# Reciprocals of softmax sums: through DRAM as rows, or spread and transposed

## The chip, the cores and the metric

The kernel runs on one core of a Trainium2 chip. The core has a matrix engine (PE, with its weight loads shown as PEld), a vector engine (DVE), a scalar engine (ACT), a general engine (POOL), and a queue that issues transfers (SP). They run side by side and wait for each other through semaphores. The metric is the device time of one execution in microseconds (us), the median over the runs; lower is better.

## The reference, cut to what matters

The program is one inference step of a two-layer encoder over 2048 prompt tokens and 64 sample tokens, with a model width of 1024. Layer 0 has two groups of heads side by side: A (eight heads, each query sees its own chunk of 64 tokens and all earlier ones) and B (eight heads, own chunk and the previous eight, with a learned bias by distance). Layer 1 has attention C (16 heads that share two key/value heads, own chunk and the previous two, with a learned sink per head). For all three:

```
p      = softmax(q k^T * scale + mask or bias)      # over the keys
o      = p v
mixed  = o * silu(gate)
h      = h + rmsnorm(mixed @ w_out) * g_post
```

The softmax is computed without its division: P = exp(s - max), and the sums of P over the keys are kept, one number per query and head. The division is made on o, at the end. This document is about how the reciprocals of these sums reach the shape in which o can be multiplied by them.

## The kernel before, in words

All work is float32. Products of high precision are built from a rounded part and a remainder, so most matmuls come in threes or pairs. The program runs five phases one after the other, with some overlap at the borders: phase 1 projects the input, phase 2 is attention A, phase 3 is attention B together with the output projection of layer 0, phase 4 projects the input of layer 1, phase 5 is attention C with the second output projection.

The scores of 128 queries lie with the queries on the 128 partitions. `exp` (L701, L1185, L1697) writes P and, as a side result, the sum of each row: one number per partition. P is then transposed block by block (L725, L1202, L1706), so that P V comes out with 64 head dimensions on partitions and queries along the free axis: `OT` holds two heads (2 x 64 partitions) by up to 512 queries. The sums therefore have their queries on partitions, while `OT` has them along the free axis.

Before, the turn is made like this. A reciprocal `ri` is taken of the sums of a group (four blocks of 128 queries, two heads, in A and B; one block of 128 queries, 16 heads, in C). A copy spreads each reciprocal 64 times along the free axis (`rb`: POOL L805 in A, ACT in B, ACT in C, POOL L1726 for the sample tokens in C). PE transposes `rb` in blocks of 128x128 (L810, L1245, L1735) into PSUM, where each of the two halves of 64 partitions now holds 64 equal rows: one head's reciprocals along the queries. DVE multiplies `OT` by that (L812, L1246, L1737). POOL multiplies by the gate `G` (L813, L1247, L1743). In A and B the result goes to DRAM (`sM`, `sMB`) for the output projection; in C it stays on chip and is split in a rounded part (`MM`, ACT) and a remainder (POOL L1750) for the projection (L963).

What sets the order of the work around it:

- In A (`finish` from L796) each group is a list of closures on the list `extra`. One entry is taken at the end of each step; a step is one block of queries of one head, or several short ones. Before, a group has two entries, `finish` and `rest`. For PE, DVE, ACT and POOL the order of the steps is written out by hand; SP's order is chosen by a planner that simulates the program. `rb` has one buffer. What is left on the lists after the last step is placed by the planner on all engines.
- In B (`finish` from L1230) each group is a generator in `J.side`. `J.rest()` resumes it once per unit (one block, one head), and once more when two or more wait. The loop `for _ in range(YR3 ...)` puts two or three turns between the spread copy and the transposes. PE, DVE, ACT and SP follow the written order; POOL is planned. The groups are `GROUPS = [(4, 4), (8, 4), (12, 4), (2, 2), (0, 2)]`, first block and count; the last two are short.
- In C (`gate` from L1715) each block of 128 queries is a generator in `J.side` too, with the same turns; the first eight steps are planned, and from then on PE, DVE, ACT and SP follow the written order, while POOL is planned. At most two blocks are open at a time (`J.open`).

The output projection's tail (L984 to L1005) runs between: DVE scales a row tile `z` by its norm and `g_post` (L994, two halves), POOL adds the residual (L1002), and SP stores it.

## Time and profile before

| | us |
|---|---|
| runs: median of 3 (lowest, highest) | 2731.71 (2725.06, 2732.81) |
| the profiled execution, its own time | 2735.98 |
| its span in the profile | 2733.9 |
| PE busy in the span | 2579.7 (94%) |
| DVE busy | 1473.2 (54%) |
| ACT busy | 1390.9 (51%) |
| POOL busy | 769.1 (28%) |

The profile shows one execution. Its span runs from the first to the last instruction and is 2.1 us shorter than the execution's own time. A group in it is a line of the code with an engine, an operation and the tiles it writes and reads (out<-in), the count after an x, the busy time, the mean duration in ns, and then the idle time of the engine just before, with what ended it. Rows with a time in front are single instructions or merged runs of them: start, length, engine, line. The chain of waits is followed back from the last instruction, at each step to what released it. "issue" in it is time in which the engine waited for nothing that the profile shows. Helper functions give their own line to all that they issue: L211 is every ACT copy, L214 every DVE remainder.

### The profile page before, as it was taken

To read this page: it belongs to the slowest core of one execution; us is meant where nothing else is said; L and a number is where in the kernel's file an instruction comes from. 1 tells how busy PE (TensorE), PEld (TensorE's weight loads), DVE (VectorE), ACT (ScalarE), POOL (GpSimd) and SP (SyncE) were. 2 spreads that over 40 slices of the span, in tenths; PEclk is the share of its full clock that TensorE was granted. 3 is DMA by queue.
4 is the path that set the end of the run, shared out by engine and by line. 5 is a ranking of instruction groups with operands and counts; after the bars stand their busy time and mean duration, and the time that the engine had idled before them with its cause. 6 is when DMAs were issued, how large, how long until landed. Compare 5 with 4: busy or idle time off the path is not lost.

```text
span 2733.9 us, 46704 instructions
## 1 busy us (share of the span) xinstructions
PE 2579.7 (94%) x16296; PEld 2355.2 (86%) x16296; DVE 1473.2 (54%) x4048; ACT 1390.9 (51%) x3547; POOL 769.1 (28%) x1311
## 2 busy tenths in 40 slices
PE   6999999999999999999988999899999999999997
PEld 6999999899998888888777888679999998787886
DVE  5542245352117878787666777545213204787884
ACT  4332242332237777777556666542233224777783
POOL 2123122113112323321200333374212220344444
PEclk9999999999999999999899999999999999999999
DMA  6456443737537666661476777666535429454552
GB/s 235 153 154 215 127 152 94 248 112 225 165 94 204 183 183 190 169 168 47 166 194 152 192 200 192 184 202 217 159 98 168 125 69 254 108 139 130 139 132 70
DMA packets 382283, 437.92 MB, mean 160 GB/s; under 512 B 49937, under 2 KB 308889, under 8 KB 378817
## 3 DMA queue, kind: packets, MB, share of 16 engines
q1 hardware_dynamic: 382048, 434.95, 54.7%
q8 instruction: 129, 2.11, 0.3%
q14 instruction: 106, 0.86, 0.1%
HBM read 282.80 MB, written 157.09 MB: 161 GB/s over the span
## 4 chain that ended last, share of the span: by engine, by line
PE 74%; DVE 11%; DMA 5%; ACT 5%; issue 3%; POOL 2%; SPq 1%; ACTq 0%; DVEq 0%; POOLq 0%
PE pm L237 36%; PE proj L963 9%; PE s L682 6%; PE acc L753 4%; PE t L725 3%; PE acc L1215 2%; DVE PT L214 2%; PE s L1175 2%; PE t L1202 2%; PE acc L1713 2%; PE t L1706 2%; PE s L1685 1%; ACT P L701 1%; DVE m L688 1%; DVE s L1688 1%
## 5 line engine op out<-in xcount | busy, mean ns | idle before, releaser
L237 PE MATMUL pm<-X,W 128*128 128x384 f32 (+2 forms) x4536 | 755.5, 325 | 1.4 <-DVE ev L214 1.0
L237 PEld LDWEIGHTS pm<-X,W 128*128 128x128 f32 x4536 | 734.9, 190 | 3.9 <-DVE ev L214 1.2
L211 ACT ACTIVATE PT<-t 128x512 fp32r<-128x512 f32 (+3 forms) x704 | 343.5, 504 | 265.5 <-PE t L1202 108.4
L214 DVE SCALAR_TENSOR_TENSOR PT<-t,PT 128x512 fp32r<-128x512 f32 (+3 forms) x688 | 375.5, 569 | 93.4 <-ACT PT L211 90.6
L963 PE MATMUL proj<-Wo,MM 128*128 128x512 f32 (+1 forms) x1368 | 379.5, 407 | 10.9 <-ACT z L211 8.8
L228 POOL TENSOR_TENSOR W<-R,W 128x768 fp32r<-128x768 f32 (+3 forms) x114 | 228.7, 2030 | 536.4 <-ACT W L227 536.1
L214 DVE SCALAR_TENSOR_TENSOR ev<-pm,ev 128x256 fp32r<-128x256 f32 (+3 forms) x197 | 98.7, 503 | 468.8 <-ACT ev L1553 169.3
L963 PEld LDWEIGHTS proj<-Wo,MM 128*128 128x128 f32 (+1 forms) x1368 | 237.1, 186 | 55.8 <-ACT z L211 12.4
L237 PE MATMUL pm<-W,X 128*128 128x256 f32 (+5 forms) x2040 | 281.1, 297 | 0.0
L237 PEld LDWEIGHTS pm<-W,X 128*128 128x128 f32 (+1 forms) x2040 | 271.7, 187 | 1.3 <-POOL W L228 0.3
L701 ACT ACTIVATE P<-s,m 128x512 f32<-128x512 f32 (+9 forms) x344 | 209.2, 616 | 32.8 <-DVE m L690 30.4
L682 PE MATMUL s<-KA,Q 128*128 128x512 f32 (+7 forms) x640 | 202.1, 398 | 9.7 <-ACT P L701 8.8
L725 PE MATMUL t<-ident,P 128*128 128x128 f32 x1088 | 177.0, 277 | 3.3 <-ACT P L701 0.8
L688 DVE TENSOR_REDUCE m<-s 128x1 f32<-128x480 f32 (+7 forms) x216 | 132.4, 613 | 82.3 <-PE s L682 81.9
L725 PEld LDWEIGHTS t<-ident,P 128*128 128x128 f32 x1088 | 135.4, 141 | 41.4 <-ACT P L701 15.0
L753 PE MATMUL acc<-PT,V 128*128 128x256 f32 x1152 | 156.0, 285 | 6.4 <-DVE OT L762 6.4
L753 PEld LDWEIGHTS acc<-PT,V 128*128 128x128 f32 x1152 | 140.4, 188 | 11.5 <-PE t L725 6.0
L1697 ACT ACTIVATE P<-s,m 128x256 f32<-128x256 f32 (+2 forms) x264 | 119.5, 465 | 10.6 <-DVE m L1689 9.3
L1688 DVE CUSTOM_DVE_ANT_0 s<-s,mask 128x256 f32<-128x256 f32 (+1 forms) x256 | 107.6, 422 | 20.2 <-PE t L1706 7.9
L1179 DVE CUSTOM_DVE_ANT_0 s<-s,bias 128x640 f32<-128x640 f32 (+4 forms) x128 | 95.1, 743 | 43.1 <-PE s L1175 41.8
L682 PE MATMUL s<-KR,Q 128*128 128x384 f32 (+6 forms) x320 | 116.7, 365 | 1.6 <-DMA Q<-sQR 1.6
L227 ACT ACTIVATE W<-R 128x768 fp32r<-128x768 f32 (+3 forms) x114 | 98.2, 909 | 38.0 <-DMA R<-in_ab_w_in_dram 19.5
(249 smaller groups left out, 4019.9 us busy)
## 6 DMA issues: line engine op xcount, KB each, us to landing
Q<-sQA SPq DMA_DIRECT2D x128, 128.0 KB, 3.2
sWO<-W SPq DMA_DIRECT2D x32, 512.0 KB, 3.8
Q<-sQB SPq DMA_DIRECT2D x128, 128.0 KB, 3.0
Wo<-sWO SPq DMA_DIRECT2D x16, 1024.0 KB, 9.0
Q<-sQC SPq DMA_DIRECT2D x32, 512.0 KB, 7.6
R<-in_ab_w_in_dram SPq DMA_DIRECT2D x40, 384.0 KB, 3.7
K<-sKB SPq DMA_DIRECT2D x56, 256.0 KB, 5.2
V<-sVB SPq DMA_DIRECT2D x24, 512.0 KB, 6.4
```

Source lines behind the costliest of these rows:

```text
L211: nc.scalar.activation(out, in_, AF.Copy)
L214: nc.vector.scalar_tensor_tensor(out, x, scale, hi, op0=ALU.mult, op1=ALU.subtract)
L228: nc.gpsimd.tensor_tensor(Wv[:, 1, k0:k1], Rv, Wv[:, 0, k0:k1], op=ALU.subtract)
L237: nc.tensor.matmul(ps, lhs(x, k), rhs(y, k), start=(j == 0), stop=(j == n - 1))
L682: nc.tensor.matmul(s[:r, :n], self.Q[:, x, self.qo:self.qo + r], rhs, start=(x == 0), stop=(x == 2))
L688: nc.vector.tensor_reduce(m[:r, j:j + 1], s[:r, :n], axis=AX.X, op=ALU.max)
L701: nc.scalar.activation(self.P[:r, o0:o0 + n], self.s.pop(j)[:r, :n], AF.Exp, bias=self.m[:r, 6:7], accum_out=acc)
L725: nc.tensor.transpose(t[:, b], self.P[:, (b0 + b) * 128:(b0 + b + 1) * 128], ident)
L753: nc.tensor.matmul(acc[:, (i // 2) % 2], H.V[:, b0 + b], PT[:, x, b], start=(b0 + b == 0 and x == 0), stop=(b0 + b == i and x == 1))
L963: nc.tensor.matmul(p, M[:, x, k, :r], W[k][:, y, cs], start=(k == k0 and t == 0), stop=(k == k1 - 1 and t == 2))
L1688: nc.vector.tensor_tensor_reduce(s[:, c, :w], s[:, c, :w], mk, 1.0, -3e38, ALU.add, ALU.max, m[:, 0, c:c + 1])
L1697: nc.scalar.activation(self.P[:, c, :w], self.s[:, c, :w], AF.Exp, bias=m[:, 1, c:c + 1], accum_out=m[:, 0, c:c + 1])
```

## The change

The reciprocals are no longer spread before the transpose. Two helpers are new. `to_rows` transposes the small block of reciprocals of a group (128 queries by up to 16 columns) once, copies the rows (8 or 16 by 128) out of PSUM on ACT, and stores them to a new scratch tensor in DRAM. `rows_to_halves` loads them back twice, once for each half of 64 partitions, with a stride of zero over the partitions, so that all 64 read the same row. `rb` then holds what the transposes held in PSUM before, but in SBUF.

In A a group has four entries on the list in place of two: `finish`, `rows`, `back`, `scale`. The last group (head pair 3, blocks 12 to 15) keeps the old form. In B the spread copy and the transposes go, and the turns are one, one and two. In C the reciprocals are taken one step earlier, in a new method `sums`, and a second list `J.recips` carries the row store and, one step later, the loads of `rb` and of `G`; `gate` then lets POOL multiply G by rb, and DVE multiply OT by that in one instruction of 128x1024, in place of two on DVE and then one on POOL. The sample tokens of C go the same way.

```
+    sRA = scratch("sRA", [4, 5, 8, 128])
+    sRB = scratch("sRB", [4, 6, 8, 128])
+    sRC = scratch("sRC", [17, 16, 128])
...
+    def to_rows(pool, pt, ri, n, dst):
+
+        p = pt.tile([128, 512], F32, name="t")
+        nc.tensor.transpose(p[:n, :128], ri, ident)
+        e = pool.tile([16, 128], F32, name="rT", bufs=1)
+        nc.scalar.activation(e[:n], p[:n, :128], AF.Copy)
+        dma(dst, e[:n])
+
+    def rows_to_halves(out, src, half, ap):
+
+        for e in range(2):
+            dma(out[e * 64:e * 64 + 64], bass.AP(tensor=src.tensor, offset=src.offset + e * half, ap=[[0, 64]] + ap))
...
-                rb = sc.tile([128, 4, 2, 64], F32, name="rb", bufs=1)
-                nc.gpsimd.tensor_copy(rb[:, :nb], ri[:, :nb, :, None].to_broadcast([128, nb, 2, 64]))
+                rb = sc.tile([128, 4, 128], F32, name="rb", bufs=1)
+                if (hp, b0) != (3, 12):
+                    sr = sRA[hp, b0 // 4, 0:2 * nb]
+
+                    def rows():
+                        to_rows(sc, ps_t, ri[:, :, :nb].rearrange("p e b -> p (e b)") if nb == 4 else ri[:, :, 0], 2 * nb, sr)
+
+                    def back():
+                        rows_to_halves(rb[:, :nb].rearrange("p b q -> p (b q)"), sr, nb * 128, [[1, nb * 128]])
+
+                    def scale():
+                        nc.vector.tensor_mul(OT[:, c0:c1], OT[:, c0:c1], rb.rearrange("p b q -> p (b q)")[:, :c1 - c0])
+                        nc.gpsimd.tensor_tensor(OT[:, c0:c1], OT[:, c0:c1], G[:, :c1 - c0], op=ALU.mult)
+                        dma(sM[hp * 128:hp * 128 + 128, c0:c1], OT[:, c0:c1])
+                    extra.extend([rows, back, scale])
+                    return
...
-                rb = sc.tile([128, 4, 2, 64], F32, name="rb", bufs=1)
-                copy(rb[:, :nb], ri[:, :nb, :, None].to_broadcast([128, nb, 2, 64]))
-                for _ in range(YR3 if t0 < 512 or t0 == SEQ else 2):
-                    yield
-                p = ps_t.tile([128, 512], F32, name="t")
-                for b in range(nb):
-                    nc.tensor.transpose(p[:, b * 128:b * 128 + 128], rb[:, b].rearrange("p a b -> p (a b)"), ident)
-                nc.vector.tensor_mul(OT[:, :n], OT[:, :n], p[:, :n])
+                yield
+                sr = sRB[hp, -(-t0 // 512), 0:2 * nb]
+                to_rows(sc, ps_t, ri[:, :2 * nb], 2 * nb, sr)
+                yield
+                rb = sc.tile([128, 512], F32, name="rb", bufs=1)
+                rows_to_halves(rb[:, :n], sr, nb * 128, [[1, n]])
+                yield
+                yield
+                nc.vector.tensor_mul(OT[:, :n], OT[:, :n], rb[:, :n])
                 nc.gpsimd.tensor_tensor(OT[:, :n], OT[:, :n], G[:, :n], op=ALU.mult)
...
+            def recips(ri, i, R):
+
+                n = ri.shape[-1]
+                r = 128 if i < 16 else DS
+                to_rows(sc, ps_t, ri, n, sRC[i, :n])
+                yield
+                R.rb = sc.tile([128, 8, 128], F32, name="rb", bufs=1)[:, :, :r]
+                rows_to_halves(R.rb, sRC[i], 8 * 128 if r == 128 else 64, [[128, 8], [1, r]])
+                R.G = qp.tile([128, 8, 128], F32, name="G")[:, :, :r]
+                dma(R.G, sGC[:, i * 128:i * 128 + r].rearrange("(j p) t -> p j t", p=128))
+                yield
+
+            def gate(OT, R, t0, r):
+
                 for _ in range(YRB if r == 128 else YRS):
                     yield
-                for g in range(2):
...
-                nc.gpsimd.tensor_tensor(OT[:, :, :r], OT[:, :, :r], G[:, :, :r], op=ALU.mult)
+                nc.gpsimd.tensor_tensor(R.G, R.G, R.rb, op=ALU.mult)
+                yield
+                nc.vector.tensor_tensor(OT, OT, R.G, op=ALU.mult)
+                yield
...
+                def sums(self):
+
+                    B = self.B
+                    ri = sc.tile([128, 16], F32, name="ri", bufs=2)
+                    nc.vector.reciprocal(ri.rearrange("p (e g c) -> p g e c", e=2, g=2), B.rs)
+                    B.R = K()
+                    J.recips.add(recips(ri, B.i, B.R))
...
+                J.recips.each()
+                if nxt and (nxt.g, nxt.e) == (1, 1):
+                    nxt.sums()
```

More of the change, by code (lines that the diff above doesn't have):

```diff
@@ L809, in rest @@
                     for b in range(nb):
-                        nc.tensor.transpose(p[:, b], rb[:, b].rearrange("p a b -> p (a b)"), ident)
+                        nc.tensor.transpose(p[:, b], rb[:, b], ident)
                     pv = p.rearrange("p b q -> p (b q)")
@@ L1656, in phase5 @@
             J.open = 0
-            J.mm = None
+            J.mm, J.recips = None, Fill()
             mask = one.tile([128, 256], F32, name="mask")
@@ L1728, in gate @@
+            def gate(OT, R, t0, r):
                 for _ in range(YRB if r == 128 else YRS):
                     yield
-                for g in range(2):
-                    t = ps_t.tile([128, 512], F32, name="t")
-                    tv = t.rearrange("p (j q) -> p j q", j=4)
-                    js = slice(g * 4, g * 4 + 4)
-                    for j in range(4):
-                        nc.tensor.transpose(tv[:, j], rbs[g][:, j].rearrange("p e d -> p (e d)"), ident)
-                    if r == 128:
-                        nc.vector.tensor_tensor(OT[:, js], OT[:, js], tv, op=ALU.mult)
-                    else:
-                        for e in range(2):
-                            er = slice(e * 64, e * 64 + 64)
-                            nc.vector.tensor_tensor(OT[er, js, :r], OT[er, js, :r], tv[er, :, er], op=ALU.mult)
-                    yield
@@ L1805, in out @@
                     if (g, e) == (1, 1):
[L1806 to L1808 removed]
+                        J.side.add(gate(B.OT, B.R, B.i * 128, 128))
+                def sums(self):
[4 more added lines that the diff above has]
+                    J.recips.add(recips(ri, B.i, B.R))
             def sample():
@@ L1841, in sample @@
                     yield
-                ri = sc.tile([128, 2, 4], F32, name="ris", bufs=1)
-                nc.vector.reciprocal(ri, rs)
-                J.side.add(gate(OT, ri, SEQ, DS))
+                ri = sc.tile([128, 8], F32, name="ris", bufs=1)
+                nc.vector.reciprocal(ri, rs.rearrange("p g c -> p (g c)"))
+                R = K()
+                yield
+                yield from recips(ri, 16, R)
+                J.side.add(gate(OT, R, SEQ, DS))
             units = [(i, g, e) for i in range(16) for g in range(2) for e in range(2)]
```

25 lines of the change are left out of this document (7 added, 18 removed).

## The prediction

> **What bounds the kernel now.** I read the busy time by stretch first, cut where the code's phases begin (attention A 800 to 1345 us, attention B to 1790, the second input projection to 2300, attention C to the end), and the shares of the chain of waits.
>
> ```profile
> PE 74%; DVE 11%; DMA 5%; ACT 5%; issue 3%; POOL 2%; SPq 1%; ACTq 0%; DVEq 0%; POOLq 0%
> 690.00:1345.00 655.00, 620.94 (x4333) 558.93 (x4333) 430.54 (x1020) 431.50 (x1131) 161.09 (x394) 0.99 0.54 152
> 1345.00:1790.00 445.00, 408.28 (x2509) 348.06 (x2510) 285.27 (x782) 272.60 (x690) 112.85 (x217) 0.95 0.71 192
> 2300.00:2700.00 400.00, 374.60 (x2126) 312.09 (x2125) 321.50 (x863) 300.09 (x902) 169.40 (x373) 0.98 0.50 128
> ```
>
> The columns after the length are PE, PEld, DVE, ACT and POOL busy, then the granted clock, the DMA share and GB/s. PE is busy 95%, 92% and 94% of the three stretches that the change touches, at a clock near 1, and carries 74% of the chain. A PE instruction taken out there is worth about its own time, as long as DVE (66%, 64%, 80% busy) does not become the next limit. Next come the groups that the change removes or shrinks:
>
> ```profile
> L810 PE MATMUL t<-ident,rb 128*128 128x128 f32 x68 | 10.7, 272 | 0.0
> L1245 PE MATMUL t<-ident,rb 128*128 128x128 f32 x68 | 12.7, 298 | 1.7 <-DVE PT L214 1.7
> L1735 PE MATMUL t<-ident,rb 128*128 128x128 f32 x136 | 20.5, 274 | 1.8 <-DVE PT L214 1.4 <-DVE OTs L1741 0.2 <-ACT rb L211 0.2
> L211 ACT ACTIVATE rb<-ri 128x512 f32<-128x512 f32 (+2 forms) x56 | 30.3, 569 | 17.2 <-DVE ri L1236 16.4 <-DVE rs L187 0.7
> L805 POOL COPY rb<-ri 128x512 f32<-128x512 f32 (+1 forms) x20 | 10.9, 547 | 71.9 <-DVE ri L801 67.9 <-PE t L810 4.0
> ```
>
> The 272 ns are the latency of one transpose; matmuls overlap. What one costs the chain is in the chain itself, here in one block of attention C (a block recurs every 24.3 us there):
>
> ```profile
> 2566.43 0.44 PE t L1735 x4
> ...
> 2571.71 0.44 PE t L1735 x4
> ...
> 2577.68 0.69 DVE PT L214
> 2578.37 0.90 DVE z L994 x2
> 2579.26 2.50 issue
> 2581.77 0.67 DVE OT L1803
> ```
>
> Four transposes take 0.44 us, so **0.11 us each**. The block is PE up to 2577, then ACT and DVE, with 2.5 us of "issue" inside the pair L994.
>
> **The change part by part.** *Transposes.* Attention A keeps one per group for 19 groups and four for the last: 68 become 23. Attention B: 68 become 24 (20 groups, 4 sample groups). Attention C: 136 become 17. That is 45, 44 and 119 fewer, at 0.11 us 5.0, 4.8 and 13.1 us of PE.
>
> *The spread copies.* POOL's L805 was off the path, and I count it at nothing: POOL is 25% busy there. ACT's copies go in B and C; each is replaced by a copy of at most 16 rows by 128 out of PSUM, for which there is no row; between 0 and the 0.57 us mean above, I take 0.25. In B, ACT waited 16.4 us for ri at the old copies; the new copy waits for a PE transpose instead. I take 2 us of gain in B (bounds -2 and 8) and nothing in C, where ACT runs behind PE.
>
> *The round trip.* Each group stores up to 8 KB and then loads two halves of 64 partitions, 128 KB each in A and B, 256 KB in C. The nearest rows are the store of a scaled group (L814), a query load of 64 partitions with 128 KB, and the load of G:
>
> ```profile
> DMA to landing us min/median/max: 1.4/2.8/6.7
> Q<-sQA SPq DMA_DIRECT2D x128, 128.0 KB, 3.2
> K<-sKB SPq DMA_DIRECT2D x56, 256.0 KB, 5.2
> G<-sGC SPq DMA_DIRECT2D x16, 512.0 KB, 8.7
> ```
>
> Store 1.4 to 2.8, two issues of about 0.6 (the four of L632, quoted next, take 2.36), landing 3.2: 5.8 to 7.2 us from the store's issue, and with about 1 us for the transpose and ACT's copy 7 to 8 us. A store at its slowest (6.7) makes it 12. Is it ready when DVE, which works in the written order, comes to the multiplication? The pace:
>
> ```profile
> 928.48 0.20 DVE L801 RECIPROCAL ri<-rsum 128x8 f32<-128x8 f32 x1
> 930.80 2.36 SPq L632 DMA_DIRECT2D KA<-sKA  x4
> 933.80 0.69 DVE L812 TENSOR_TENSOR OT<-OT,t 128x512 f32<-128x512 f32 x1 [0.22 <-PE t L810]
> 945.34 0.20 DVE L801 RECIPROCAL ri<-rsum 128x8 f32<-128x8 f32 x1
> ...
> 1741.21 0.18 DVE L1236 RECIPROCAL ri<-rsum 128x4 f32<-128x4 f32 x1
> 1747.19 0.40 DVE L1246 TENSOR_TENSOR OT<-OT,t 128x256 f32<-128x256 f32 x1
> 1751.36 0.18 DVE L1236 RECIPROCAL ri<-rsum 128x4 f32<-128x4 f32 x1
> ```
>
> In A a group takes one entry per step: 933.80 is where the row transpose goes, and the multiplication comes two steps later, near 945. That is 11 us for 8: enough, except where the next head's loads (L632 onwards) stand in the same SP queue and fill the rings, as they do here. I take 5 us of DVE waits that reach PE over the 19 groups (bounds 0 and 30). In B a finish has three turns between transpose and multiplication. In the short groups at the end, three turns took 6.0 us (1741.21 to 1747.19), and a finish now needs six turns where four steps pass, so turns come in pairs: 6 us for 7 to 8. Eight finishes there lose 1 us or so each, of which DVE's 36% idle time hides a part: 5 us (bounds 0 and 25). In the long groups a turn is a step, and 445 us over 136 units make a step of 3.3 us: 10 us, enough. The first tile of the output projection also becomes ready some two turns later, at a point where PE has gaps: 2 us (0 to 4). In C the transpose comes three steps (18 us of a block's 24.3) before the use: stores, halves (5.2) and G behind them (8.7) take 17 at most, and are hidden. SP's new waits hold the loads behind them; those have a block (C) or a group (B) in hand, so nothing, or if the cover is gone the price of the last rival.
>
> *Between A and B.* The last group of A keeps the old form, but its rb shares one buffer with the group before. It used to wait for that group's transposes:
>
> ```profile
> 1341.02 0.44 PE t L810 x4
> ...
> 1345.62 0.70 DVE OT L812
> ...
> 1346.37 0.67 PE t L1298 x4
> ```
>
> Now it waits for that group's multiplication: transpose at 1341.1, copy 1341.7, store landed 1343.5 to 1345, halves landed 1347 to 1349, multiplication, POOL's copy, four transposes and the last multiplication behind it: 1349.7 to 1351.7 where 1346.3 stood. PE's L1298 starts when that is done, so 3.4 to 5.4: I take 4.4 (down to 0, if the planner finds other work).
>
> *The multiplications.* They read rb from SBUF in place of PSUM. In C, POOL's product becomes G by rb, early, and DVE does one 128x1024 product with two SBUF inputs:
>
> ```profile
> L996 DVE TENSOR_TENSOR x<-z,x x4: 691/692/693, 1857.0 to 2730.2; 128x512 f32<-128x512 f32 x4
> L994 DVE SCALAR_TENSOR_TENSOR z<-z,rs,g_post x68: 700/744/2910, 1522.3 to 2729.4; 128x512 f32<-128x512 f32 x64, 64x512 f32<-64x512 f32 x4
> 2569.97 0.16 DVE L1689 SCALAR_TENSOR_TENSOR m<-m,nsink 128x4 f32<-128x4 f32 x1
> ...
> 2573.88 0.63 DVE L1737 TENSOR_TENSOR OT<-OT,t 128x512 f32<-128x512 f32 x1
> 2574.59 2.39 POOL L1743 TENSOR_TENSOR OT<-OT,G 128x1024 f32<-128x1024 f32 x1 [4.18 <-DVE OT L1737]
> 2576.51 0.49 DVE L1689 SCALAR_TENSOR_TENSOR m<-m,nsink 128x4 f32<-128x4 f32 x1
> 2577.54 1.05 ACT L211 ACTIVATE MM<-OT 128x1024 fp32r<-128x1024 f32 x1
> 2578.28 3.56 DVE L994 SCALAR_TENSOR_TENSOR z<-z,rs,g_post 128x512 f32<-128x512 f32 x2
> 2578.67 2.63 POOL L1750 TENSOR_TENSOR MM<-OT,MM 128x1024 fp32r<-128x1024 f32 x1 [1.37 <-ACT MM L211]
> ```
>
> From 0.69 us for 512 columns and 0.40 for 256 (1747.19), 1024 take 1.27 us against the old pair of 0.63. The important reading is L994: two of 0.74 take 3.56, because the second stands until POOL's L1750 ends; L1689, with POOL's L1743 beside it, takes 0.49 in place of 0.16. So DVE with two SBUF inputs waits for POOL. The block's end is then set by: MM copy, L1750, second z. With two sets of transposes gone and one transpose added, the MM copy and L1750 come 0.77 us earlier, L1750 at 2577.9. The first z must start before that to keep its place. DVE reaches it 0.44 earlier (one set), 0.17 for the reciprocal that moves away, 0.33 for L1689 that stands free, and 0.64 later for the longer product: 2578.0 where it was 2578.28. **A tie.** If the first z wins, each of 14 blocks gains 0.77 us, 10.8 in all; if it loses, both z wait, and the 0.7 us comes back: nothing. I take 5.
>
> The Trainium skill (SBUF — State Buffer, § Who interferes with whom) states that a Vector instruction with two SBUF inputs contends with a GpSimd instruction that reads SBUF, and that the later one blocks until the other ends. The rows above show it for scalar_tensor_tensor; no run here shows it for the tensor_tensor that this change makes. By the page the 39 new products of A and B would each wait behind POOL (25% busy, ops of about 1.3 us: an estimate of 0.2 us, 6 us in all, part hidden); by the PSUM rows they would not; the sum leaves it out.
>
> *The end of C.* POOL's last products stood on the chain:
>
> ```profile
> 2693.65 2.85 POOL L1743 TENSOR_TENSOR OT<-OT,G 128x1024 f32<-128x1024 f32 x1 [5.86 <-DVE OT L1737]
> ...
> 2701.93 5.33 PE L963 MATMUL proj<-Wo,MM 128*128 128x512 f32 x22 [1.51 <-POOL MM L1750]
> ```
>
> followed by the MM copy and L1750, for which PE waited 1.51 us. G by rb is done before OT now; 2.85 less 0.6 for the longer product on DVE, and four transposes: 3.5 with the PE idle time that ends (bounds 0 and 5).
>
> **The sum.** -5.0 +5 (A), +4.4 (between), -4.8 -2 +5 +2 (B), -5 -3.5 (C): -3.9 us on the profiled execution's own 2735.98, so 2732.1; that execution stood 4.3 above the median of the runs, so **2728 us**.
>
> **The rivals.**
> 1. *Waits hidden, tie won.* For it: PE is the bound by the chain, and 8 us fit into the 11 and 10 of most groups. Both: -5 -6.8 +4.4 -10.8 -3.5 = -21.7, 2710; the tie alone 2722, the waits alone 2716. Against it: the loads in the rings at 930, the pairs of turns.
> 2. *Late rows in DVE's order* (slower). The multiplication stands in DVE's fixed order; behind it wait the next maxima (L688, L1179), then ACT's exponentials, then PE. The forecast has 10 us over 39 groups, 0.26 each. It is slower from 0.57 us each; at 0.8, 31 us: 2749. For it: stores up to 6.7 us. Against: most of A's and B's groups have 2 to 3 us to spare.
> 3. *SP held.* A half's load waits on SP until its store has landed, 1.4 to 6.7 us, and the next heads' keys and values queue behind it. If those are late by 3 us at three heads of A and half of that at the 16 groups of loads of B half the time: 9 + 12 above the forecast, less what DVE hides: 2741. Against: they start a group early.
> 4. *The change does not do what it says on the path*: PE's gaps only grow, since DVE, ACT and POOL keep the pace; then C gives 3.5 and B nothing, within 0.3%.
>
> **How the numbers follow.** The forecast, own range 2724 to 2738, has 0.38, the fourth 0.05; the first 0.34; the second 0.17, the third 0.06. A difference of 0.3% (8.2 us, about the spread of the runs before) is what can be told from none: faster 0.34, same 0.43, slower 0.23. 8 in 10 reach from 2711, where the first rival's best half ends, to 2746, short of the second's price.
>
> **What would show it.** Right: 0.11 us steps and 64 transposes by rb; L1298 some 4 us later behind the end of A; waits of DVE's product for DMA in A only where L632 loads stand, and in B's short groups. The tie shows in the block's length in C: 24.3 or 23.5. Wrong: DVE waiting for rb at most groups (second rival); PE waiting for loads of K, V or Q (third); no such waits at all and blocks of 23.5 (first).

## The result, and the profile after

The changed kernel takes 2802.8 us (median of four runs, 2801.6 to 2813.4) where the kernel before takes 2732.1: the ratio is 1.027, 95% interval 1.025 to 1.030. The forecast was 2728, its range ended at 2746. The change makes the kernel 71 us slower, and every stage that it touches has a part in that.

The first view is four groups of PE by source line, in the kernel before and then in the one after: the transposes of attention A's weights, those of the sample's keys in attention B, and the value products of B and C. Behind the count stand the shortest, median and longest duration in ns, then the starts of the first and the last instruction.

```profile
L725 PE MATMUL t<-ident,P x1088: 270/272/421, 805.7 to 1338.3; 128*128 128x128 f32 x182
L1298 PE MATMUL t<-ident,x x16: 271/372/421, 1346.4 to 1441.7; 128*128 128x128 f32 x16
L1215 PE MATMUL acc<-PT,V x672: 274/282/580, 1351.3 to 1779.6; 128*128 128x256 f32 x168
L1713 PE MATMUL acc<-PT,VC x248: 387/397/794, 2293.6 to 2689.6; 128*128 128x512 f32 x124
```

```profile
L742 PE MATMUL t<-ident,P x1088: 270/272/421, 802.3 to 1335.1; 128*128 128x128 f32 x182
L1333 PE MATMUL t<-ident,x x16: 273/417/421, 1346.8 to 1448.4; 128*128 128x128 f32 x16
L1248 PE MATMUL acc<-PT,V x672: 274/282/580, 1352.3 to 1799.7; 128*128 128x256 f32 x168
L1748 PE MATMUL acc<-PT,VC x248: 387/397/795, 2317.4 to 2756.5; 128*128 128x512 f32 x124
```

A's transposes take as long as before (532.6 and 532.8 us), though they start 3.4 us earlier. From A's last to B's first transposes it is 11.7 us in place of 8.1. B, from 1346.8 to 1799.7, takes 452.9 in place of 433.2. C's value products spread over 439.1 us in place of 396.0. So some 4, 20 and 43 us: the loss has three places, and most of it lies in C.

In C one block shows it all. These are instructions of DVE, ACT, POOL and PE in order of time (start, duration, and in brackets how long the engine stood idle and what ended that):

```profile
2571.45 1.23 DVE L1768 TENSOR_TENSOR OT<-OT,G 128x1024 f32<-128x1024 f32 x1
...
2574.84 1.05 ACT L228 ACTIVATE MM<-OT 128x1024 fp32r<-128x1024 f32 x1
2575.96 3.55 DVE L1027 SCALAR_TENSOR_TENSOR z<-z,rs,g_post 128x512 f32<-128x512 f32 x2
2576.19 2.77 POOL L1766 TENSOR_TENSOR G<-G,rb 128x1024 f32<-128x1024 f32 x1 [3.15 <-DMA G<-sGC]
2579.53 2.34 POOL L1776 TENSOR_TENSOR MM<-OT,MM 128x1024 fp32r<-128x1024 f32 x1
2581.90 0.68 DVE L1829 TENSOR_TENSOR OT<-acc,tbm 64x512 f32<-64x512 f32 x1 [2.38 <-POOL MM L1776]
2582.73 2.04 PE L1748 MATMUL acc<-PT,VC 128*128 128x512 f32 x4 [3.57 <-DVE OT L1829]
```

"The residual" is from here on the remainder MM<-OT,MM that POOL makes behind ACT's copy of MM (L1776 here, L1750 before the change); POOL's addition to the residual stream (L1002) is another instruction. The product G by rb (L1766, 2576.19) belongs to the *next* block: DVE multiplies by it a whole block later. POOL's order is not written by hand in this stage, and the planner put that product ahead of this block's residual L1776. There POOL stands 3.15 us until G has landed, then multiplies for 2.77 us, and the residual starts 3.64 us after ACT's copy of MM has ended (2575.89). Before the change it started 0.08 us after it in nearly every block (copy to 2578.59, L1750 at 2578.67). The residual gives back the buffer OT, L1829 waits for that, and PE's next value products wait 3.57 us for L1829.

After this wait PE is slow as well. The mean granted clock is the third column from the right; first the stretch behind the same place before the change, then after:

```profile
2580.00:2586.00 6.00, 5.15 (x36) 4.25 (x34) 5.68 (x13) 4.17 (x14) 4.41 (x6) 1.00 0.77 181
```

```profile
2584.00:2590.00 6.00, 6.00 (x26) 5.30 (x26) 4.31 (x15) 4.29 (x14) 1.85 (x10) 0.60 0.48 175
```

In six busy microseconds PE starts 26 matmuls, at a clock of 0.60; before the change it started 36 in 5.15. So a block pays for PE's wait, and for slow work behind it.

In B the groups of the sample's stretch show the other mechanism. These are ACT's copy of a group's rows, SP's queue behind it, and DVE's multiplication:

```profile
1392.13 0.27 ACT L219 ACTIVATE rT<-t 8x128 f32<-8x128 f32 x1
1392.43 0.28 SPq L220 DMA_DIRECT2D sRB<-rT  x1
1392.81 2.55 SPq L208 DMA_DIRECT2D Q<-sQB  x4
1395.40 1.23 SPq L1144 DMA_DIRECT2D K<-sKB  x2
1396.68 0.59 SPq L1179 DMA_DIRECT2D V<-sVB  x1
1397.37 1.18 SPq L225 DMA_DIRECT2D rb<-sRB  x2
...
1405.13 0.69 DVE L1281 TENSOR_TENSOR OT<-OT,rb 128x512 f32<-128x512 f32 x1 [6.17 <-DMA rb<-sRB]
```

The next heads' seven loads stand in SP's queue between the store and the halves: the halves leave 4.94 us behind the store, with seven transfers ahead of them, and DVE can multiply 12.7 us after the store and not 6 to 7. DVE stands 6.17 us for it.

### The profile page after: what moved, and what is told of

Read it like the earlier page. It is cut to its first block, busy times and chain, and to the rows that moved or that the text cites. A ratio compares the mean times of both kernels' runs of the same rounds, so it can differ in the third digit from the quotient of the medians.

```text
span 2799.8 us, 46651 instructions
## 1 busy us (share of the span) xinstructions
PE 2578.6 (92%) x16088; PEld 2347.7 (84%) x16088; DVE 1459.1 (52%) x4029; ACT 1375.4 (49%) x3551; POOL 765.8 (27%) x1288
## 4 chain that ended last, share of the span: by engine, by line
PE 72%; DMA 9%; DVE 8%; ACT 4%; issue 3%; POOL 2%; SPq 1%; ACTq 0%; DVEq 0%; POOLq 0%
PE pm L254 37%; PE proj L996 7%; PE s L699 6%; PE acc L770 4%; PE t L742 3%; PE acc L1748 2%; PE acc L1248 2%; PE s L1720 2%; PE s L1208 2%; DVE PT L231 2%; PE t L1741 2%; PE t L1235 1%; DMA rb<-sRB 1%; ACT P L718 1%; DMA G<-sGC 1%
## 5 line engine op out<-in xcount | busy, mean ns | idle before, releaser
L770 PE MATMUL acc<-PT,V 128*128 128x256 f32 x1152 | 155.7, 285 | 6.7 <-DVE OT L779 6.7
L1748 PE MATMUL acc<-PT,VC 128*128 128x512 f32 x248 | 80.1, 441 | 49.0 <-DVE OT L1829 44.5
L1248 PE MATMUL acc<-PT,V 128*128 128x256 f32 x672 | 115.1, 304 | 8.2 <-DVE rs L191 4.5
L1723 DVE CUSTOM_DVE_ANT_0 s<-s,mask 128x256 f32<-128x256 f32 (+1 forms) x256 | 107.6, 422 | 24.3 <-PE t L1741 11.6
```

The lines of the kernel that those rows point to most:

```text
L770: nc.tensor.matmul(acc[:, (i // 2) % 2], H.V[:, b0 + b], PT[:, x, b], start=(b0 + b == 0 and x == 0), stop=(b0 + b == i and x == 1))
L1248: nc.tensor.matmul(acc, self.H.V[:, self.base - self.H.b0 + b], self.PT[:, x, off + b], start=(b == 0 and x == 0), stop=(b == nblk - 1 and ...
L1748: nc.tensor.matmul(acc, V, PT[:kk, x], start=(first and x == 0), stop=(last and x == 1))
```

## The experiments

Seventeen kernels ran. Times are against runs of the kernel before on the same chip; a ratio of 1.001 is 2.7 us. The stages are measured in each profile as above (starts of PE's groups): A's first to last score, the border (A's last transposes to B's first ones of the sample's keys), B to its last value product, and what follows.

| run | ratio, 95% interval | A | border | B | then to the end |
|---|---|---|---|---|---|
| before | 1 | 529.1 | 8.1 | 433.2 | 954.3 |
| after | 1.027, 1.025 to 1.030 | 529.3 | 11.7 | 452.9 | 1000.1 |
| 1 only A changed | 1.0027, 1.0012 to 1.0041 | 528.0 | 11.6 | 433.2 | 952.5 |
| 2 only B | 1.0093, 1.0068 to 1.0119 | 525.9 | 8.0 | 454.5 | 956.1 |
| 3 only C | 1.0131, 1.0108 to 1.0154 | 526.6 | 8.0 | 426.4 | 991.7 |
| 4 C, loads later | 1.0057, 1.0035 to 1.0078 | 527.6 | 8.0 | 437.0 | 971.9 |
| 5 C, G first | 1.0032, 1.0012 to 1.0051 | 526.2 | 8.0 | 431.9 | 960.6 |
| 6 C, G first, halves later | 1.0064, 1.0041 to 1.0088 | 526.3 | 8.0 | 430.2 | 977.4 |
| 7 B, halves behind the store | 1.0027, 1.0005 to 1.0049 | 525.5 | 8.0 | 435.5 | 954.5 |
| 8 as 7, multiplied a turn earlier | 1.0139, 1.0103 to 1.0174 | 527.4 | 8.0 | 460.6 | 958.0 |
| 9 A, two old groups last | 1.0049, 1.0033 to 1.0065 | 529.7 | 14.4 | 424.1 | 962.1 |
| 10 as 9, rows copied by DVE | 1.0020, 1.0006 to 1.0035 | 522.8 | 14.9 | 430.1 | 956.2 |
| 11 C, G first, halves behind the store | 1.0002, 0.9991 to 1.0014 | 525.9 | 8.0 | 427.8 | 958.3 |
| 12 A of 10, B of 7, C of 11 | 1.0074, 1.0059 to 1.0089 | 525.1 | 15.3 | 440.2 | 965.5 |
| 13 A, all groups new, DVE copies | 1.0036, 1.0019 to 1.0053 | 522.4 | 10.1 | 443.7 | 954.2 |
| 14 C, product held back, blocks 4 to 13 | 0.9986, 0.9970 to 1.0002 | 526.2 | 8.0 | 430.4 | 952.5 |
| 15 as 7, rows copied by DVE | 1.0035, 1.0019 to 1.0052 | 524.4 | 8.0 | 437.3 | 953.3 |
| 16 A of 13, B before, C of 14 | 1.0036, 1.0022 to 1.0049 | 524.8 | 10.3 | 447.1 | 949.2 |
| 17 as 14, blocks 1 to 14 | 0.9983, 0.9969 to 0.9997 | 526.3 | 8.0 | 429.4 | 951.9 |

Each row of stages is one profile. Stages in their old form differ between profiles: A lies between 524.4 and 529.1, B between 424 and 437 (leaving out runs 13 and 16, whose A ends in another way). The ratios decide, and the columns say where.

**Runs 1 to 3: one stage at a time.** The edit is the change's own, kept in one stage and undone in the other two.

> Only attention A has the rows by way of DRAM; attention B and C are those of the kernel before. Theory (each stage has its own loss, read from the two traces): A from its first score to its last takes 529.3 us with the change and 529.2 without, and the first transposes of B (L1298 before, L1333 after) follow 11.6 us behind A's last transposes in place of 8.2; so +3.4 us over the kernel before, ratio about 1.001. Rival 1 (A gains its 5 us of PE, and B's start gives them back): PE in A ends 4 to 5 us earlier, time -1 to -2. Rival 2 (the stages push each other: A's late results make B's loss): +10 to +20.

> Only attention B has the rows by way of DRAM. Theory: B's own loss, which is 20 us between its first L1298 and its last value product (433.0 us before, 452.9 after), is all there: +18 to +24 us, and DVE waits for rb about 12 times, 30 us in all, most of them between 1385 and 1495 us where the sample's groups and the first quad's finish. Rival (B's loss comes from A's late border group, whose store and loads stand at B's start): under +8 us.

> Only attention C has the rows by way of DRAM. Theory (order on POOL): +42 to +48 us, all of it C's own; POOL waits some 3 us a block for G at the product G by rb, which stands ahead of the residual of MM for the block before, and PE waits some 3 to 4 us a block for OT. Rival (C suffers from where B left its loads and its output projection): under +30 us.

The ratios give +7, +25 and +36 us, together 68 of the 71: the stages have each their own loss, and neither rival that made one stage answer for another holds. A's is twice what I expected; 3.5 us of it are the border, and A itself, 528.0 us in this profile, lies within the spread of the old form. B's is one above my bounds, C's is below my bounds and above the rival's. Two waits of the third run (2300 to 2720 us), in us in total, times, and the longest:

```profile
POOL G L1748 <- DMA G<-sGC: 46.5, 14, 4.9
PE acc L1730 <- DVE OT L1811: 42.5, 17, 3.8
```

**Runs 4 to 6 and 11: C.** Run 4 issues the halves and G one step later:

```diff
 to_rows(sc, ps_t, ri, n, sRC[i, :n])
-yield
+for _ in range(2 if i in BLOCKS5[4:15] else 1):
+    yield
```

> As the run with only C changed, but SP issues the two halves of rb and G one step (some 6 us) later for blocks 5 to 15; their product is then in POOL's queue behind the residual of MM instead of ahead of it. Nothing is left out. Theory (order on POOL): the residual no longer stands behind G's landing and a 2.4 us product; blocks go from some 27.5 back to 24 to 25 us, and the whole is within +0 to +15 us of the kernel before. Rival D (the 1.23 us product with two SBUF inputs on DVE, and its lock with POOL, make the loss): unchanged, +40 to +48. Rival L (the transfers come late, and a still later issue makes it worse): above +50.

The product now stood behind the residual, and +36 fell to +16 us, one beyond the theory's bound. Rivals D and L are out as the main cause. In the second half of the stage blocks took 25.1 to 25.5 us; POOL now waited for G in front of its own small instructions, which the row statistics and DVE behind them need (38 us in all, up to 7.9).

Run 5 leaves the product where it was and loads G earlier; run 6 does both:

```diff
 def recips(ri, i, R):
+    R.G = qp.tile([128, 8, 128], F32, name="G")[:, :, :r]
+    dma(R.G, sGC[...])
     to_rows(sc, ps_t, ri, n, sRC[i, :n])
...
-    R.G = qp.tile(...)
-    dma(R.G, sGC[...])
```

> Only attention C changed, as in the third run, but G is loaded ahead of the transpose, a step before rb, in place of behind rb; the product G by rb keeps its place in POOL's queue ahead of the residual of MM. Theory (order on POOL): POOL's wait in front of the product, 3.3 us a block for G, becomes one for rb, whose halves are issued 1.2 us before G was: about 1 to 2 us shorter, and the 2.4 us product stays ahead of the residual. Blocks of 25.5 to 26.5 us, +18 to +28 us over the kernel before. Rival (only the wait hurts, not the product's place): +0 to +10. Rival L (512 KB of G is no longer the late one, rb is late anyway behind the ring's other loads): +30 to +36 as without the edit.

> Attention C with both edits: G loaded ahead of the transpose, and the halves of rb one step later, so that the product stands behind the residual of MM. The fourth run (halves and G later) left +16 us, with POOL waiting 1.0 to 1.4 us (7.9 at most) for G in front of the product and the row sums' statistics behind it. Theory: that wait falls to that for rb, which is issued 1.1 us before G was and is half its size per load; POOL waits under 0.5 us a block, the block is 24 to 24.6 us, and the whole within -5 to +6 us of the kernel before. Rival D (DVE's 1.23 us product or its lock keeps the rest): +12 to +16 again.

Run 5 was better than my theory allowed (+9), run 6 worse (+17, one above rival D's range; but run 11, next, keeps D's product and loses nothing). Run 5's +9 lies in the range of its rival "only the wait hurts", but not for that reason. A block of run 5:

```profile
2553.04 2.40 POOL L1748 TENSOR_TENSOR G<-G,rb 128x1024 f32<-128x1024 f32 x1 [5.81 <-DMA rb<-sRC]
2553.91 1.05 ACT L228 ACTIVATE MM<-OT 128x1024 fp32r<-128x1024 f32 x1
...
2555.69 2.43 POOL L1758 TENSOR_TENSOR MM<-OT,MM 128x1024 fp32r<-128x1024 f32 x1
```

POOL waits longer here than in the block above (5.81 us against 3.15), and it costs little: the residual starts 0.73 us behind the copy (2554.96). So neither POOL's wait nor the product's place is by itself the price. It is how late the residual starts (2.5 to 4.2 us in most blocks of run 3), and, when the product stands behind the residual as in runs 4 and 6, what it holds up there. Run 6 issued the halves later; POOL's waits for rb came to 36 us in only 7 pieces, up to 9.5 us long.

Run 11 tests that form of the theory: G first, and the halves right behind the store (both `yield`s moved below the loads), so that the product is done before the residual's turn.

> Only attention C changed; G loaded ahead of the transpose as in the fifth run, and the halves of rb issued right behind the store of their rows, ahead of the values VC, whose load waits some 3 us for PE in the same queue. Theory (what counts is how late the residual of MM starts behind its copy: 2.96 us with C as changed, 0.73 with G first, 0.08 before the change): the halves are issued 1 to 1.6 us earlier, the product G by rb ends before the copy of MM does, the residual starts within 0.2 us of it; blocks of 23.9 to 24.5 us, -6 to +3 us against the kernel before. Rival (SP, standing for the store, makes VC, KC or Q late): +8 or more. Rival D (DVE's longer product): +6 to +10 as with G first.

The ratio is 1.0002. In 7 of 13 blocks the residual now waits for ACT's copy alone. One of the others shows what the prediction had left open, whether DVE's tensor_tensor with two SBUF inputs waits for POOL:

```profile
2545.14 2.42 POOL L1748 TENSOR_TENSOR G<-G,rb 128x1024 f32<-128x1024 f32 x1 [2.75 <-DMA rb<-sRC]
2545.67 2.96 DVE L1750 TENSOR_TENSOR OT<-OT,G 128x1024 f32<-128x1024 f32 x1
```

DVE's product, 1.23 us alone, takes 2.96 and ends 1.07 after POOL's. It does wait.

**Runs 14 and 17: the product held back by a dependence.** DVE copies one element of G onto itself, in its written order, a step before it needs the product; POOL cannot take the product up earlier.

```diff
+if t0 // 128 in BLOCKS5[4:14]:
+    nc.vector.tensor_copy(R.G[0:1, 0, 0:1], R.G[0:1, 0, 0:1])
 nc.gpsimd.tensor_tensor(R.G, R.G, R.rb, op=ALU.mult)
```

> Only attention C changed, G loaded ahead of the transpose, and for blocks 4 to 13 DVE copies one element of G onto itself in its written order a step before it needs the product: the product G by rb can then not be put into POOL's queue ahead of the residual of MM for the block before, where it stood till now, and comes some 18 us after its loads were issued. Nothing is left out. Theory (what counts is that nothing of the next block stands in front of the residual): POOL waits for no DMA there, the residual starts within 0.3 us of its copy; blocks of 23.6 to 24.3 us, -10 to 0 us against the kernel before. Rival D (DVE's 1.23 us product, and its lock with POOL, keep a part): +3 to +10. Rival (the product, 2.4 us in front of POOL's small softmax instructions, delays the exponentials): +5 or more, with ACT waiting for POOL's m.

> As the fourteenth run (-3.7 us, interval -8.2 to +0.5), with DVE's one-element copy for blocks 1 to 14 in place of 4 to 13, so that the product G by rb of the first and the last blocks leaves the place ahead of the residual too. Theory: those five blocks gain what the nine gained, up to 0.3 us each against the old form: -3 to -8 us against the kernel before. Rival (the ends of the stage are set by other waits, the leftover projection and the last tiles): the same as the fourteenth run within 2 us.

```profile
2547.40 2.42 POOL L1760 TENSOR_TENSOR MM<-OT,MM 128x1024 fp32r<-128x1024 f32 x1 [0.84 <-ACT MM L228]
...
2560.49 0.13 DVE L1749 COPY G<-G 1x1 f32<-1x1 f32 x1
2560.69 2.40 POOL L1750 TENSOR_TENSOR G<-G,rb 128x1024 f32<-128x1024 f32 x1 [0.77 <-DVE G L1749]
2566.92 1.23 DVE L1752 TENSOR_TENSOR OT<-OT,G 128x1024 f32<-128x1024 f32 x1
2570.31 1.05 ACT L228 ACTIVATE MM<-OT 128x1024 fp32r<-128x1024 f32 x1
2571.43 3.64 DVE L1011 SCALAR_TENSOR_TENSOR z<-z,rs,g_post 128x512 f32<-128x512 f32 x2
2571.44 2.43 POOL L1760 TENSOR_TENSOR MM<-OT,MM 128x1024 fp32r<-128x1024 f32 x1 [0.84 <-DMA KC<-sKC]
```

The product lies in the middle of the block, and the residual follows its copy at 0.08 us, here as in ten of the thirteen blocks between the first and the last two. (The last bracket names a load of keys; that the start lies 0.08 us behind the copy's end, as in the other blocks, says that the copy released it.) From residual to residual it is 24.04 us (2547.40 to 2571.44) where the kernel before takes 24.3. Runs 14 and 17 are 4 and 5 us faster than the kernel before; the seventeenth's interval lies just below 1, the fourteenth's reaches just above it. This is the only form of the change that beats the kernel before, by 0.17%. The difference between the two runs is within what either expectation allowed. The gain isn't spread evenly, and not all of it comes from fewer transposes: the two blocks around 2500 us take 43.1 us in place of 48.9 with the same work but for the transposes by rb (some 1.5 us), and it is there that the kernel before has a late residual of its own (2507.43, 3.26 us behind its copy; 0.17 or 0.18 us in runs 14 and 17); and the stage's beginning loses it again, with the second residual of run 14 107.6 us after the first score in place of 99.0. Why the beginning is longer is not shown.

**Runs 7, 8 and 15: B.** Run 7 issues the halves right behind the store; run 8 then takes out one `yield` ahead of the multiplication; run 15 is run 7 with the rows copied by DVE.

```diff
 to_rows(sc, ps_t, ri[:, :2 * nb], 2 * nb, sr)
-yield
 rb = sc.tile([128, 512], F32, name="rb", bufs=1)
 rows_to_halves(rb[:, :n], sr, nb * 128, [[1, n]])
 yield
 yield
+yield        # taken out again in run 8
 nc.vector.tensor_mul(OT[:, :n], OT[:, :n], rb[:, :n])
```

> Only attention B changed, and the two halves are issued right behind the store of their rows, before the next heads' seven loads, and not behind them; the multiplication keeps its turn. Theory (place in SP's queue): rows land at 1396.7 where the store left at 1384.4, 12.2 us, of which 4.2 are the issues of Q, K and V in between and some 4 us their bytes ahead in the rings; without them some 7 us; DVE's waits for rb fall from 31.6 to under 10 us, the sample stretch loses some 3 us instead of 10. What OT's buffer waits for (sMB<-OT, 17.6 us at the end of B) stays: +8 to +15 us over the kernel before in place of +26. Rival (SP, standing for the store, delays Q, K, V so that PE waits for them): +20 or more, with PE waiting for DMA Q or K.

> As the run before it, and the multiplication one turn earlier, so that a group's buffer OT is given back about as early as in the kernel before. Theory: the waits of OT for its store at the end of B (17.6 us) halve; DVE's waits for rb are longer than in the run before, since 3 to 6 us less lie between: +4 to +12 us. Rival (rb's landing is what decides): +15 or more, DVE's waits for rb above 20 us.

> Only attention B changed, halves issued right behind the store as in the seventh run (+7 us), and the rows copied out of PSUM by DVE in place of ACT, which waited 17.2 us there for the row transposes. Theory (as in A, ACT's wait in the written order is what is left): 2 to 5 us less, +1 to +6 against the kernel before. Rival (DVE has the waits for rb already, and gets one more): +7 to +12.

```profile
1382.07 0.28 SPq L220 DMA_DIRECT2D sRB<-rT  x1
1383.42 1.09 SPq L225 DMA_DIRECT2D rb<-sRB  x2
1384.55 2.52 SPq L208 DMA_DIRECT2D Q<-sQB  x4
...
1388.52 0.68 DVE L1265 TENSOR_TENSOR OT<-OT,rb 128x512 f32<-128x512 f32 x1
```

In run 7 the halves leave 1.35 us behind the store, the multiplication 6.45 us behind it finds them there, and DVE's waits for rb (to 1800 us) fall from 31.6 to 11.9 us, not quite under 10. +25 falls to +7, one better than my bounds: the place in SP's queue is B's main cause. SP's standing for the store isn't free, though. PE now waits for loads in B, among them for the sample's cached keys and the next heads' keys:

```profile
PE t L1317 <- DMA x<-in_cache_b_k_dram: 4.1, 2, 3.4
PE s L1192 <- DMA K<-sKB: 3.4, 1, 3.4
```

With 1.2 us for Q that is 8.7 us, where run 2 has 2.2 and for the kernel before none is listed: the sign that the rival named, at a smaller size. Run 8 went the rival's way (+38): with one turn less DVE waits for rb 56.7 us, so the OT buffers that I wanted back earlier are not worth it. Run 15 did too: DVE's wait for the row transpose is 8.8 us where ACT's was 17.2, yet the time did not fall (1.0035). ACT's wait is not what is left in B. What is left of B, 7 us, is not settled. PE's waits for loads (8.7 us in run 7, 8.2 in run 15) have the right size; OT's waits for its store (18.6 us in run 7, 19.3 in run 15, none before) are DVE's and another candidate. No run tried either by itself.

**Runs 9, 10 and 13: A.** Run 9 gives the old form to the last two groups instead of the last one, run 10 also copies the rows by DVE, run 13 has DVE's copy and no group of the old form.

```diff
-if (hp, b0) != (3, 12):
+if (hp, b0) not in ((3, 8), (3, 12)):       # run 13: if True:
...
-nc.scalar.activation(e[:n], p[:n, :128], AF.Copy)
+nc.vector.tensor_copy(e[:n], p[:n, :128])   # runs 10 and 13
```

> Only attention A changed, and the last-but-one group (pair 3, blocks 8 to 11) keeps the old form too, so that the buffer rb of the last group is given back by transposes again and not by a multiplication that waits for DRAM. Theory: the first transposes of B follow 8.1 us behind A's last ones, as before the change, in place of 11.6; of the +7 us that the first run measured for A alone (interval +3.3 to +11.2) 3.5 go: +1 to +6. Rival (the border is paid back by B's first steps anyway, which wait for other work): still +5 to +9.

> As the run before it, and the 16 x 128 rows are copied out of PSUM by DVE in place of ACT. Theory (ACT stands in the written order for the row transpose: 20.3 us over 17 groups, and hands back there the 5 us that PE gains): DVE has its own next work, the maxima, behind PE's next scores anyway; A from first to last score falls from some 528.5 to 524 to 526 us; 3 to 5 us less than the run before. Rival 4 of the prediction (PE's gaps only grow, whoever copies): A as long as in the run before, time the same within 2 us.

> Only attention A changed, rows copied out of PSUM by DVE, and all 20 groups by way of DRAM, the last one too: no group of the old form is left behind one of the new. Theory (at the border POOL's spread copy of the first old group waits, in one shared buffer, for the multiplication of the last new group, which waits for DRAM; two old groups made it 14.4 us in place of 11.6): B's first transposes follow A's last ones by some 8 us or less again, since PE has one row transpose there and no more; with A some 3 us shorter, -6 to 0 us against the kernel before. Rival (the last multiplication, which now waits for DRAM at the border, holds DVE's first work of B): +4 to +8.

Run 9 contradicted me: it is 13 us slower than the kernel before, above both ranges, and the border grew to 14.4 us. The changed kernel's border, and then run 9's:

```profile
1343.25 0.69 DVE L832 TENSOR_TENSOR OT<-OT,rb 128x512 f32<-128x512 f32 x1 [1.07 <-DMA rb<-sRA]
...
1345.22 0.61 POOL L837 COPY rb<-ri 128x512 f32<-128x512 f32 x1
...
1345.89 1.12 PE L843 MATMUL t<-ident,rb 128*128 128x128 f32 x4 [5.14 <-POOL rb L837]
```

```profile
1346.48 0.69 DVE L832 TENSOR_TENSOR OT<-OT,rb 128x512 f32<-128x512 f32 x1 [1.93 <-DMA rb<-sRA]
...
1348.46 0.61 POOL L837 COPY rb<-ri 128x512 f32<-128x512 f32 x1
...
1349.12 1.11 PE L843 MATMUL t<-ident,rb 128*128 128x128 f32 x4 [6.11 <-POOL rb L837]
```

Wherever an old group follows a new one, its spread copy waits in the shared buffer for the new one's multiplication and so for DRAM (and on POOL for that group's product with the gate), and PE waits for the copy. With two old groups PE waits 6.11 us in place of 5.14, and then for a second copy and with four more transposes. A buffer of its own for the last group, which should remove this wait, wasn't tried. Run 13 removes the old form and the border shrinks to 10.1, but B grows to 443.7; run 16 shows the same (10.3 and 447.1). The time is +10 us, above even the rival's range. The rival's mechanism is there: the last multiplications wait for DRAM in DVE's order (4.9 us in three waits), and PE's first transposes of B wait 4.41 us for a row copy that DVE does behind one of them. But PE also waits for loads, which the rival didn't have:

```profile
PE proj L996 <- DMA Wo<-sWO: 6.3, 3, 3.8
PE s L1208 <- DMA K<-sKB: 3.8, 1, 3.8
```

The first weights Wo of the output projection leave SP 14.7 us behind B's first transposes, after the last round trips, where they left 4.2 us behind them before the change and PE waited for no load in B. In run 16 the wait for Wo is 9.6 us. How much of B's growth each part makes is not shown. Run 10 against run 9 confirms the theory on ACT: A falls from 529.7 to 522.8 us and the time by 0.0029, some 8 us, for the one moved copy. The two waits, of run 1 and of run 10:

```profile
ACT rT L219 <- PE t L217: 20.3, 17, 3.1
```

```profile
DVE rT L219 <- PE t L217: 3.4, 4, 1.3
```

**Runs 12 and 16: together.**

> All three stages with the rows by way of DRAM and all repairs: A as in the tenth run, B as in the seventh (halves right behind the store), C as in the eleventh. Theory (each stage has its own loss, and they add): A -4 to +2, B +2 to +10, C -6 to +3: -8 to +12 us against the kernel before, that is 60 to 80 us faster than the changed kernel. Rival (the repairs push each other, SP's waits above all): above +15.

> A as in the thirteenth run, B as before the change, C as in the fourteenth: the stages add, so that the time is the sum of their two differences; -12 to +2 us against the kernel before. If they do not add (A's end and C lie 900 us apart, with all of B and the second input projection between), the difference between the sum and this run shows it.

Run 12 gives +20 us where runs 10, 7 and 11 add to 13; run 16 gives +10 where runs 13 and 14 add to 6. Run 16's interval (+6 to +13) holds its sum. Run 12's (+16 to +24) does not hold 13, and its time is in the rival's range and not in mine; but that sum of three runs is itself uncertain by some 8 us, so that the repaired stages cost each other anything is likely and not shown. Its border is the longest of all (15.3), and its B, 440.2, longer than that of runs 7 and 15; why is not shown.

## Why the prediction was wrong

The direction was wrong and the range missed by 57 us. By its steps:

*"POOL's product becomes G by rb, early", counted at nothing, and "hidden" for C's round trip: this step failed: C's terms add to -8.5 us, and +36 came.* Hidden it is for DVE, which uses the product a block later. But the prediction costed the transfer against the written orders alone. POOL has none there. An instruction with a distant use can be planned to any place, and this one came to stand, waiting for a load, ahead of the one POOL instruction on the block's chain, L1750 in the old kernel, which the prediction itself had named as what sets the block's end. With the residual back in its place (runs 11, 14), C loses nothing.

*The round trip of 7 to 8 us: right for the transfers, wrong for B's queue.* With nothing in between it fits within 6.45 us of the store (run 7). In B the prediction looked for short spacing in the last eight finishes and counted the rest as "10 us, enough". The sample's stretch at B's beginning has two finishes under way at once, and there the side queue is pumped twice a step, so turns come in pairs there too; and the halves stood behind seven loads. The prediction had the loads in the queue for A, where they were harmless (DVE waited 1.1 us for rb in A, and 2.6 at the border), and not for B: 5 us of waits were said and +0.2 for B as a whole, and 25 came. The second rival (late rows in DVE's order) is what happened in B, for the third rival's reason, with the halves late in SP's queue in place of the keys. Once the halves stand ahead of the keys (run 7), PE waits for loads, as the third rival had it.

*ACT's copies.* In B a gain of 2 was taken, in A nothing. In A the 0.27 us copy made ACT stand 20.3 us in its order, and A did not get the 5 us of PE that the transposes freed there; with the copy on DVE A takes 522.4 to 525.1 us where the old form takes 524.4 to 529.1 and ACT's copy 528.0 to 529.7.

*The border, +4.4: right* in place and mechanism, and near in size, 3.5 us by the trace.

*119 transposes fewer in C, 13.1 us of PE, and the tie of z: PE's time is saved, the block's mostly not.* In the steady blocks of run 14 the residual waits for no load. One block, from residual to residual, in the kernel before and then in run 14 (length, then PE, PEld, DVE, ACT and POOL busy):

```profile
2578.67:2603.02 24.35, 23.50 (x137) 19.87 (x136) 21.39 (x56) 19.18 (x58) 11.33 (x25) 1.00 0.58 142
```

```profile
2571.44:2595.47 24.03, 22.75 (x130) 19.11 (x129) 21.04 (x57) 18.37 (x57) 11.24 (x25) 1.00 0.61 166
```

PE's busy time falls by 0.75 us, as the 0.77 of the prediction had it, but the block by 0.32: the rest is longer idling of PE, which waits 1.17 us for OT where it waited 0.71. The tie came out as one (z starts at 2571.43, the residual at 2571.44), and the z pair still takes 3.64. The fourth rival (PE's gaps only grow) holds for more than half of it. This points to the ring of DVE, ACT and POOL as C's limit, which is argued and not tested; the first reading, that PE work there is worth its own time, was too simple. For A that reading used a row from 690 us on, 110 us ahead of A: from 800 us on DVE is busy 78% and not 66%.

*The lock.* The rule of the Trainium skill (SBUF — State Buffer, § Who interferes with whom) that the prediction weighed holds for the tensor_tensor too, by the 2.96 us of run 11. The estimate of 6 us for the 39 products of A and B did not come: they take 0.58 and 0.60 us in the mean, since POOL seldom works beside them: in the changed kernel beside none of A's 19, and in B beside three of 24 (the sample's four small ones included).

## What to carry to other kernels

A transfer is hidden from the engine that uses it, not from the engine that must touch it first: for each instruction that waits for a new load, find what is planned or written behind it on the same engine, and whether that lies on the chain. The store and the loads of a round trip belong next to each other in their queue, ahead of bulk loads; look then for who waits for the bulk loads that this holds back. The copy out of PSUM belongs on an engine that would wait for PE anyway (it paid in A, and made no difference in B). And when PE shares a stage with a ring of other engines that nearly fills the same time, an edit of PE may be worth less than PE's own time: price what the ring would then do.

## What the hardware did that was not expected

A wait of PE of some 2 to 4 us often costs more than itself. Eight matmuls of scores in C (L1720 or its like) take 1.12 us where the granted clock is 1.00 (before, at 2579.63) and 2.06 where it is 0.50 (both cases below). For each wait of PE for OT in C between 2380 and 2680 us in seven of the profiles (before, after, runs 3, 4, 5, 11, 14), this counts the cases in which the next eight scores took 1.4 us or more:

```
PE's wait, us     cases   next scores slow
under 1.8           50          0
1.8 to 2.6          15          4
2.8 to 4.3          21         20
```

Two cases: one from run 5, and in the kernel after the scores that follow the wait of 3.57 us in the block shown with the result:

```profile
2560.07 1.28 PE L1730 MATMUL acc<-PT,VC 128*128 128x512 f32 x4 [1.82 <-DVE OT L1811]
...
2561.86 2.06 PE L1702 MATMUL s<-KC,Q 128*128 128x256 f32 x8
```

```profile
2585.28 2.06 PE L1720 MATMUL s<-KC,Q 128*128 128x256 f32 x8
```

The Trainium skill (TensorE: Matmul & The Clock Gate, Part 1: The HAM clock gate) has the clock fall to half after an idle window of about 3.4 us. The trace agrees in kind, and shows it from 1.82 us of wait in some cases and from 2.8 in nearly all. That fits C's prices: a residual 0.73 us late (run 5) cost the stage some 9 us over 14 blocks, and one 3 us late (run 3) some 36; no run took the clock's part away by itself.
